# Prices of TensorE products taken from the trace, and new order offsets, in the list scheduler of a two-layer hybrid backbone

## The chip, the cores and the metric

The kernel runs on one core of one Trainium2 chip. The metric is the time of one execution on the device in microseconds (us); the time before is the median of three runs. The profile shows one execution of the kernel. Its engines are called PE (TensorE's matrix products), PEld (its weight loads, which overlap the products), DVE (VectorE), ACT (ScalarE), POOL (GpSimd) and SP (SyncE, which here issues the transfers).

## The reference

A backbone of two layers over 512 latent tokens with a context of 256 tokens, of width 1024. Cut to what matters:

```python
h, hc = x, ctx
for i in range(2):
    sh1, sc1, g1, sh2, sc2, g2 = split(silu(c) @ mod_w[i] + mod_b[i], 6)
    a = rmsnorm(h, norm1_w[i]) * (1 + sc1) + sh1
    if i == 0:      # the context ac is modulated in the same way with c_ctx
        m = ab_mixer(a, ac, ...)
    else:
        m = hyena_mixer(a, ...)      # two gated long convolutions, through an FFT
    h = h + g1 * m
    u = rmsnorm(h, norm2_w[i]) * (1 + sc2) + sh2
    h = h + g2 * ((silu(u @ w1) * (u @ w3)) @ w2)      # 1024 -> 2816 -> 1024
return rmsnorm(h, final_norm_w)

# ab_mixer: p = a @ w_in, then four heads of a gated delta rule (GDN) and four of
# gated linear attention (GLA), in both directions, in chunks of 64 tokens:
lmat = strict_lower(kb @ k.T * decay) + eye(64)                 # GDN, per chunk
sol = triangular_solve(lmat, concat([v * beta, kb * exp(gc)]))
s_new = s * gl + kd.T @ (u0 - kcd @ s)                          # chunk after chunk
m = concat([norm(o_gdn) * silu(z), norm(o_gla) * silu(g)]) @ w_out
```

## The kernel before

All products keep nearly the accuracy of float32 although most of them run in a shorter format (float32r): `split` (line 763) writes an operand as a rounded part on ACT and the rest on DVE, by a subtraction, and `mm3` (768) makes three products out of one. So each product of a projection stands three times in the instructions, and each weight that comes from memory costs an ACT cast and a DVE subtraction before PE can use it (`wsplit` 787, `wslab` 793). Weights are cut into slabs of 128 columns; the products of a projection are 128x512 (latent tokens) and 128x256 (context tokens). The small products of the first layer, in the block inverses, the scans and the linear attention, stay in float32 and are 32x32 to 128x128.

The work is recorded in sections, each with a name. In the first layer the string `AB_ORDER` (84) gives the order of recording, and `step` in `ab` (1153) calls what belongs to each letter: `g` the gates, `n0` to `n3` the projections of the GDN heads (`gdn_in` 1276), `p0` to `p3` their preparation, `i0` the inverse of the triangular 64x64 blocks of heads 0 and 1 and `i2` that of heads 2 and 3 (`gdn_inverse` 1331, which builds 32x32 blocks on DVE and merges them on PE in `gdn_merge` 1365, by products of 32x32 and then of 64x64), `s0` to `s3` the scans over the chunks (`gdn_scan` 1436), `l0` and `l1` the projections of the linear attention for two heads each (1528), `h0` to `h3` its heads (`gla_head` 1564), and `z0` to `z7` the projections of the output gates. Ahead of the first layer come the modulation vectors (`mlp`, `modc`, `m00` and so on), the norms (`in`) and the filters of the long convolution (`f0` to `f3`). Behind it come `out` (the output projection, `proj_late` 1685), `ffn0`, `ffn0b`, the convolution layer (`p0h` to `p3h`, `v0h` to `v3h`, `hyout`), `ffn1` and `last`.

The recorded order is not the order of issue. The class `Recorder` (229) keeps every instruction as an operation with its sources. `cost` (374) gives each a duration, `schedule` (413) is a list scheduler: it walks through time, and whenever an engine is free it gives it that one of its ready operations with the longest chain of work behind it, shifted by an offset. The offsets stand in the table `BOOST` (33), in nanoseconds, one per section and one per section and engine; they were found by a search. `clock` (428), inside `schedule`, turns the cost of a PE operation into a duration by a model of PE's clock with two levels, full and half. Where this model sees PE idle for more than `KEEP` = 900 ns (223), `warm` (567) puts products of a tile of ones by itself there, 128x128 in float32; I call them fillers. `issue` (578) then issues everything in the order found. Each engine works off its own queue in that order, so an instruction that waits holds back all behind it on its engine. Since everything is issued at one place, every instruction of an engine has line 591 in the profile, and instructions are told apart by their shapes.

The model's price of a PE operation before:

```python
            c = n / 2.4 * (1 if f32r else 2 if name == "transpose" else 4)
            op.cost += c / 4 if "tile_position" in k and k["lhsT"].shape[0] == P else c
```

Here `n` is the number of columns. `tile_position` marks products that use only a part of PE's array, such as the 32x32 pieces.

## Time and profile before

| what | value |
|---|---|
| median of three runs | 1661.76 us (1657.3 to 1662.93) |
| span of the profiled execution | 1659.7 us |
| time of the profiled execution | the profile gives its span alone; it is 2.1 us under the median |
| PE products | 8760 |
| mean memory traffic (HBM) | 121 GB/s |
| granted PE clock, mean over the span | 0.972 |

The span is the time from the first to the last instruction of the profiled execution. The clock is given as a share of the full speed of 2.4 GHz, so 0.50 is the lower level of 1.2 GHz and a mean in between says for which share of a stretch each level held. Idle time of an engine is put down to the operation that released it last. In rows of single engines a group that is named by one shape may hold other shapes that follow it without a pause.

### The profile page before, as it was taken

How to read it: one execution, taken by the hardware profiler on the slowest of the kernel's cores; microseconds unless marked ns; L12 is line 12 of the kernel's file. 1: busy time of each engine (PE TensorE's matmuls, PEld its weight loads, DVE VectorE, ACT ScalarE, POOL GpSimd, SP SyncE). 2: the span in 40 equal slices, each digit the busy share in tenths (PEclk: the TensorE clock that was granted, in tenths of full speed). 3: DMA queues.
4: the chain of work that ended last, by engine and by line, in shares of the span. 5: the costliest groups of instructions: out<-in, count | busy, mean ns of one | idle time of the engine just before them, and what ended most of it. 6: DMA issues, size and time to landing. Idle time of an engine off the chain costs nothing.

```text
span 1659.7 us, 22542 instructions
## 1 busy us (share of the span) xinstructions
PE 1607.0 (97%) x8760; PEld 1307.0 (79%) x8760; DVE 992.3 (60%) x1584; ACT 631.3 (38%) x1021; POOL 311.9 (19%) x395
## 2 busy tenths in 40 slices
PE   7999999999998899999999999999999999999998
PEld 4677777889876677888878887888887788888886
DVE  4967885587668877333376376689885433333224
ACT  4555633752546334232323224334335332222223
POOL 0334525723333200000000000244340000000002
PEclk9999997999998799999999999999999999999999
DMA  8755351221111165333378493333432233334232
GB/s 295 244 164 166 116 181 55 59 71 52 46 42 48 45 190 177 98 93 99 92 250 267 137 294 108 105 109 96 139 97 76 81 97 92 99 89 140 89 93 85
DMA packets 237540, 202.40 MB, mean 122 GB/s; under 512 B 11038, under 2 KB 211672, under 8 KB 237433
## 3 DMA queue, kind: packets, MB, share of 16 engines
q1 hardware_dynamic: 237432, 200.96, 39.5%
q8 instruction: 69, 1.13, 0.3%
q14 instruction: 39, 0.31, 0.1%
HBM read 187.27 MB, written 13.66 MB: 121 GB/s over the span
## 4 chain that ended last, share of the span: by engine, by line
PE 81%; DVE 9%; DMA 4%; ACT 2%; issue 2%; POOL 1%; SPq 1%; POOLq 0%; DVEq 0%; ACTq 0%
PE bank L591 81%; DVE t L591 9%; ACT t L591 2%; DMA t<-in_mod_w_dram 2%; POOL t L591 1%; DMA t<-in_hy_filt_out_dram 1%; SPq L591 1%; DMA t<-in_dft_filt_dram 0%; DMA kscr<-t 0%; DMA t<-in_ctx_dram 0%; DMA t<-kscr 0%; ACT bank L591 0%; POOLq L2084 0%; ACT L584 0%; DVEq L591 0%
## 5 line engine op out<-in xcount | busy, mean ns | idle before, releaser
L591 PE MATMUL bank<-t 128*128 128x512 f32 (+6 forms) x8760 | 1607.0, 354 | 45.4 <-DVE t L591 24.3
L591 PEld LDWEIGHTS bank<-t 128*128 128x128 f32 (+4 forms) x8760 | 1307.0, 183 | 344.9 <-DVE t L591 40.7
L591 DVE TENSOR_TENSOR t<-t 128x512 fp32r<-128x512 f32 (+13 forms) x707 | 534.2, 783 | 331.9 <-ACT t L591 294.4
L591 ACT CAST t<-t 128x1024 fp32r<-128x1024 f32 (+3 forms) x411 | 320.7, 794 | 728.5 <-PE bank L591 610.6
L591 POOL TENSOR_TENSOR t<-t 128x256 f32<-128x256 f32 (+3 forms) x195 | 211.7, 1106 | 740.8 <-DVE t L591 375.0
L591 DVE TENSOR_TENSOR t<-bank,t 128x512 f32<-128x512 f32 (+6 forms) x229 | 108.1, 505 | 55.5 <-PE bank L591 48.5
L591 ACT ACTIVATE t<-t 128x512 f32<-128x512 f32 (+6 forms) x183 | 114.3, 649 | 60.4 <-DVE t L591 44.1
L591 POOL COPY t<-t 32x192 f32<-32x192 f32 (+3 forms) x96 | 47.0, 496 | 479.6 <-DVE t L591 458.5
L591 DVE SCALAR_TENSOR_TENSOR t<-bank,t 128x511 f32<-128x511 f32 (+3 forms) x160 | 95.9, 617 | 55.1 <-PE bank L591 45.5
L591 DVE SCALAR_TENSOR_TENSOR t<-t 128x1024 f32<-128x1024 f32 (+8 forms) x135 | 109.9, 845 | 17.8 <-DMA t<-in_mod_w_dram 13.5
L591 DVE TENSOR_TENSOR t<-t,bank 128x512 f32<-128x512 f32 x44 | 30.2, 687 | 133.0 <-PE bank L591 132.3
L591 ACT COPY t<-bank 128x256 f32<-128x256 f32 (+4 forms) x152 | 64.9, 448 | 102.0 <-PE bank L591 99.7
L591 ACT ACTIVATE t<-bank 128x512 f32<-128x512 f32 (+7 forms) x134 | 59.8, 456 | 80.0 <-PE bank L591 76.0
L591 ACT ACTIVATE t<-bank,t 128x512 f32<-128x512 f32 (+2 forms) x87 | 48.1, 568 | 34.8 <-PE bank L591 17.3
L591 DVE SCALAR_TENSOR_TENSOR t<-t,bank 64x128 f32<-64x128 f32 (+1 forms) x112 | 38.3, 345 | 19.4 <-PE bank L591 17.0
L591 DVE COPY t<-bank 128x256 f32<-128x256 f32 (+7 forms) x68 | 29.9, 451 | 22.6 <-PE bank L591 21.0
L584 ACT ACT_TABLE_LOAD x32 | 41.1, 1283 | 1.4 <-PEq L2076 0.8
L591 POOL TENSOR_SCALAR t<-t 128x128 f32<-128x128 f32 x40 | 28.7, 725 | 48.7 <-PE bank L591 22.2
L591 DVE TENSOR_SCALAR t<-t 128x1024 f32<-128x1024 f32 (+6 forms) x52 | 25.1, 496 | 12.5 <-PE bank L591 7.3
L591 POOL MEMSET t<- 32x192 f32 (+10 forms) x47 | 18.4, 395 | 60.2 <-DVE t L591 30.1
L591 DVE TENSOR_TENSOR_SCAN t<-t 64x768 f32<-64x768 f32 x8 | 14.0, 1751 | 0.2
L591 DVE STREAM_TRANSPOSE t<-t 128x1024 f32<-128x1024 f32 x6 | 10.5, 1801 | 3.1 <-DMA kscr<-t 3.0
(17 smaller groups left out, 45.2 us busy)
## 6 DMA issues: line engine op xcount, KB each, us to landing
t<-in_ffn_w_dram SPq DMA_DIRECT2D x126, 512.0 KB
t<-in_mod_w_dram SPq DMA_DIRECT2D x96, 512.0 KB
t<-in_ab_w_in_dram SPq DMA_DIRECT2D x28, 512.0 KB
t<-in_hy_w_in_dram SPq DMA_DIRECT2D x24, 512.0 KB
kscr<-t SPq DMA_DIRECT2D x72, 128.0 KB
t<-kscr SPq DMA_DIRECT2D x24, 256.0 KB
t<-gscr SPq DMA_DIRECT2D x8, 384.0 KB
t<-in_ffn_w_dram SPq DMA_DIRECT2D x8, 384.0 KB
```

Of the source, the lines that this page charges most:

```text
L584: s.nc.scalar.add_instruction(mybir.InstLoadActFuncSet(name=s.nc.get_next_instruction_name(), engine=mybir.EngineType.Activation, act_func ...
L591: r = getattr(getattr(s.nc, o.eng), name)(*[b(x) for x in a], **{n: b(x) for n, x in k.items()})
```

## The change

`cost` prices a PE operation by other formulas: a product costs at least the load of its weights, a float32 product counts as two passes, and the small products get prices of their own. In `schedule` the surcharge of 2.5 ns a call is gone (the new prices hold one). The table `BOOST` is new throughout. Five docstrings are removed, which moves no instruction. The operations recorded are the same 5950 with the same sources and the same places in memory; their order is another, and there are 86 fillers instead of 73 (at the start, before the first layer, 50 instead of 29; in the last heads of the first layer 14 instead of 16; behind the first layer 22 instead of 28).

```diff
-BOOST = {"c": 1100, "c@gpsimd": -8900, "c@sync": 7100, "dft": 4200, "dft@scalar": -1200, "dft@vector": -316700,
...
+BOOST = {"": -47100, "@gpsimd": -2500, "@vector": -12200, "c": -4400, "c@gpsimd": -76900, "dft": 118900,
...
@@ cost
             f32r = x is not None and not isinstance(x, View) and x.dtype == F32R
             if x is not None and not isinstance(x, View):
                 op.rows = min(op.rows, x.shape[0])
-            c = n / 2.4 * (1 if f32r else 2 if name == "transpose" else 4)
-            op.cost += c / 4 if "tile_position" in k and k["lhsT"].shape[0] == P else c
+            l = k["in_"] if name == "transpose" else k["lhsT"]
+            w = l.shape[0] if name == "transpose" else int(np.prod(l.shape[1:]))
+            load = w / 1.2 + 2.5
+            if name == "transpose":
+                c = max(load, n * 0.8868)
+            elif f32r:
+                c = max(load, n * 0.4434 + 4.5)
+            else:
+                c = 2.0 * max(load, n * 0.8868 + 4.5)
+            if "tile_position" in k:
+                if l.shape[0] == P:
+                    c = 0.4434 * n
+                else:
+                    c = max(64.0, 0.9 * (n + 64.0))
+            op.cost += c
@@ schedule
-                o.end = clock(t, c + 2.5 * len(o.calls), o.rows / 128.0)
+                o.end = clock(t, c, o.rows / 128.0)
```

**The order on PE, in the inverse of heads 0 and 1.** The next rows are PE's, in the first layer, at `i0`. Products of 32x32 and 64x64 are those of the inverse, 128x512 and 128x256 are the projection of head 2 (`n2`), 128x128 the scan of head 0 (`s0`). `bank_` names the PSUM bank that is written. Before:

```order
L591 MATMUL bank_62<-t 128x512 x15
L591 MATMUL bank_65<-t 32x32 x12
L591 MATMUL bank_63<-t 32x32 x12
L591 MATMUL bank_67<-t 32x32 x12
L591 MATMUL bank_65<-t 32x32 x18
L591 MATMUL bank_63<-t 32x32 x18
L591 MATMUL bank_67<-t 64x64 x6
```

Fifteen wide products come first, then 72 of 32x32 in one run. In the new order the inverse is in two pieces. Its first half is mixed with the projection:

```order
L613 MATMUL bank_60<-t 64x64 x6
L613 MATMUL bank_61<-t 128x512 x3
L613 MATMUL bank_67<-t 64x64 x6
L613 MATMUL bank_61<-t 128x512 x6
L613 MATMUL bank_66<-t 128x128
L613 MATMUL bank_60<-t 128x128
```

Ahead of these rows the pieces of 24 and 36 products of 32x32 have six wide ones between them. The second half is mixed with the scan's 128x128 products:

```order
L613 MATMUL bank_67<-t 128x128
L613 MATMUL bank_66<-t 128x128
L613 MATMUL bank_60<-t 32x32 x12
L613 MATMUL bank_65<-t 128x128
L613 MATMUL bank_64<-t 128x128
L613 MATMUL bank_67<-t 32x32 x18
L613 MATMUL bank_66<-t 128x128
L613 MATMUL bank_60<-t 128x128
L613 MATMUL bank_61<-t 128x512 x3
```

What moved: wide products that stood ahead of the inverse, or behind it, now stand between its pieces, and a part of the scan too.

**The order on PE, in the inverse of heads 2 and 3.** PE's rows at `i2`, with the same shapes; the 128x512 products are `l0`'s and the 128x128 ones the scan of head 2. Before:

```order
L591 MATMUL bank_66<-t 32x32 x18
L591 MATMUL bank_64<-t 64x64 x6
L591 MATMUL bank_66<-t 128x128
L591 MATMUL bank_61<-t 128x128
L591 MATMUL bank_66<-t 64x64 x6
L591 MATMUL bank_67<-t 128x128
L591 MATMUL bank_64<-t 128x128
L591 MATMUL bank_61<-t 64x64 x6
L591 MATMUL bank_66<-t 64x64 x6
L591 MATMUL bank_67<-t 128x128
L591 MATMUL bank_64<-t 128x128
L591 MATMUL bank_61<-t 128x512 x3
```

Now:

```order
L613 MATMUL bank_63<-t 64x64 x6
L613 MATMUL bank_61<-t 128x128
L613 MATMUL bank_66<-t 64x64 x6
L613 MATMUL bank_65<-t 128x512 x3
L613 MATMUL bank_63<-t 64x64 x6
L613 MATMUL bank_66<-t 128x128
L613 MATMUL bank_61<-t 128x128
L613 MATMUL bank_65<-t 128x512 x3
```

What moved: three wide products at a time come between the small ones, and a group of three 128x512 and three 128x256 stands between the earlier pieces, where none stood in the rows before until the last.

**The order on DVE, at the end of head 3 and in the linear attention's head 0.** In the next rows SCALAR_TENSOR_TENSOR 64x768 is a scan of head 0 (the trace calls it a scan too), TENSOR_TENSOR 128x512 the squares of head 3 for its norm, COPY 64x12 and 64x8 the boundary copies of head 0. Before:

```order
L591 TENSOR_SCALAR t<-bank_64 128x512
L591 TENSOR_SCALAR t<-bank_62 128x256
L591 SCALAR_TENSOR_TENSOR t<-bank_65,t 128x128
L591 SCALAR_TENSOR_TENSOR t<-t 128x768
L591 TENSOR_TENSOR t<-t 128x1024
L591 SCALAR_TENSOR_TENSOR t<-t 64x768 x2
L591 TENSOR_TENSOR t<-t 128x512
L591 COPY t<-t 64x12 x2
L591 COPY t<-t 64x8 x2
L591 TENSOR_TENSOR t<-t 128x768
```

Now:

```order
L613 TENSOR_SCALAR t<-bank_61 128x512
L613 TENSOR_SCALAR t<-bank_65 128x256
L613 TENSOR_TENSOR t<-t 128x512
L613 SCALAR_TENSOR_TENSOR t<-t 128x768
L613 TENSOR_TENSOR t<-t 128x1024
L613 SCALAR_TENSOR_TENSOR t<-t 64x768 x2
L613 COPY t<-t 64x12
L613 COPY t<-t 64x8
```

What moved: the squares of head 3 from behind the two scans of head 0 to ahead of them, and two copies of the four were taken apart.

## Rows read from the trace of the kernel before

In rows of a table by stretch the columns are the stretch, its length, the busy time and the number of instructions of PE, PEld, DVE, ACT and POOL, the granted PE clock, the busy share of the DMA engines, and GB/s. In a timeline they are the start, the length, the engine, line and operation (output, sources, shape, count), and in brackets the idle time ahead with its releaser. In groups by shape they are line, engine, operation, tiles, shape, count, then busy us, mean ns of one record, and the idle time ahead.

**Rows 1.** The head of the profile and the busy times of the engines.

```profile
span 1659.7 us, 22542 instructions
...
PE 1607.0 (97%) x8760; PEld 1307.0 (79%) x8760; DVE 992.3 (60%) x1584; ACT 631.3 (38%) x1021; POOL 311.9 (19%) x395
```

**Rows 2.** The table of stretches, all engines.

```profile
0.00:86.00 86.00, 73.94 (x497) 47.70 (x497) 60.33 (x140) 42.98 (x91) 18.04 (x26) 0.94 0.84 266
268.00:274.00 6.00, 6.00 (x152) 5.33 (x151) 4.74 (x8) 1.81 (x5) 4.35 (x13) 0.98 0.07 21
274.00:294.00 20.00, 20.00 (x184) 17.22 (x182) 7.16 (x14) 7.12 (x18) 7.12 (x16) 0.50 0.17 41
399.00:418.00 19.00, 18.10 (x334) 15.92 (x334) 8.93 (x13) 6.03 (x17) 11.19 (x29) 1.00 0.01 3
418.00:437.00 19.00, 16.82 (x105) 14.66 (x106) 9.70 (x23) 10.84 (x25) 9.48 (x14) 0.82 0.21 56
516.00:530.00 14.00, 14.00 (x37) 9.50 (x37) 10.32 (x20) 3.52 (x7) 0.09 (x1) 0.51 0.09 27
547.00:571.00 24.00, 19.65 (x92) 16.82 (x93) 19.40 (x46) 5.83 (x9) 4.73 (x4) 0.58 0.18 55
584.00:877.00 293.00, 291.74 (x1284) 233.17 (x1285) 149.81 (x164) 90.21 (x114) 0.00 (x0) 1.00 0.48 147
1286.00:1652.00 366.00, 365.64 (x1584) 295.96 (x1582) 123.11 (x141) 103.45 (x139) 10.77 (x7) 1.00 0.31 95
```

**Rows 3.** Timeline of PE, 250 to 585 us.

```profile
260.85 91.68 PE L591 MATMUL bank<-t 128*128 128x256 f32 x763 [1.36 <-DVE t L591]
...
418.48 0.49 PE L591 MATMUL bank<-t 128*128 128x128 f32 x2 [0.99 <-ACT t L591]
419.48 15.68 PE L591 MATMUL bank<-t 128*128 128x128 f32 x98 [0.51 <-ACT t L591]
...
458.23 17.36 PE L591 MATMUL bank<-t 128*128 128x128 f32 x127 [2.14 <-DVE t L591]
...
498.67 5.26 PE L591 MATMUL bank<-t 128*128 128x512 f32 x20 [1.19 <-DVE t L591]
...
537.42 4.63 PE L591 MATMUL bank<-t 64*128 64x128 f32 x28 [1.34 <-DVE t L591]
```

**Rows 4.** PE by shape: 268 to 274, 274 to 294, 399 to 418 us.

```profile
L591 PE MATMUL bank<-t 32*32 32x32 f32 x143 | 4.2, 194 | 0.0
L591 PE MATMUL bank<-t 128*128 128x512 f32 x9 | 2.3, 397 | 0.0
...
L591 PE MATMUL bank<-t 64*64 64x64 f32 x55 | 6.5, 316 | 0.0
L591 PE MATMUL bank<-t 32*32 32x32 f32 x102 | 5.5, 237 | 0.0
L591 PE MATMUL bank<-t 128*128 128x512 f32 x9 | 4.9, 681 | 0.0
L591 PE MATMUL bank<-t 128*128 128x128 f32 x18 | 4.8, 439 | 0.0
...
L591 PE MATMUL bank<-t 128*128 128x512 f32 x15 | 6.0, 429 | 0.0
L591 PE MATMUL bank<-t 128*128 128x256 f32 x15 | 4.2, 280 | 0.0
```

**Rows 5.** The table of stretches, a stretch of eight fillers and one of wide products alone.

```profile
30.00:33.57 3.57, 3.57 (x17) 3.57 (x17) 3.47 (x6) 1.64 (x4) 0.00 (x0) 0.50 1.02 397
705.00:747.00 42.00, 42.00 (x184) 34.28 (x183) 14.33 (x16) 12.74 (x16) 0.00 (x0) 1.00 0.32 94
```

**Rows 6.** Timeline of DVE, 490 to 500 and 530 to 585 us.

```profile
494.37 3.53 DVE L591 TENSOR_TENSOR_SCAN t<-t 64x768 f32<-64x768 f32 x2
...
532.46 0.96 DVE L591 TENSOR_TENSOR t<-t 128x768 fp32r<-128x768 f32 x1
545.89 2.38 DVE L591 TENSOR_TENSOR t<-t 128x768 fp32r<-128x768 f32 x1
```

More of the change, by code (lines that the diff above doesn't have):

```diff
@@ L32 @@
 CW = 256
-BOOST = {"c": 1100, "c@gpsimd": -8900, "c@sync": 7100, "dft": 4200, "dft@scalar": -1200, "dft@vector": -316700,
[5 rows of a table removed]
-         "g": 119000, "g@gpsimd": 1100, "g@scalar": -1900, "g@sync": -17900, "g@tensor": 5500, "h": -119600,
-         "h0": -2100, "h0@gpsimd": -54600, "h0@scalar": 24800, "h0@tensor": 1200, "h0@vector": 2700,
-         "h1@scalar": 34600, "h2": 4200, "h2@gpsimd": 145500, "h2@scalar": -3900, "h2@tensor": 22100,
-         "h3@gpsimd": 6800, "h@vector": -200, "ht@scalar": 11900, "ht@tensor": 89700, "hy": -14100,
-         "hy@sync": -12500, "hy@vector": 2100, "hyout@scalar": 26400, "hyout@sync": 4000, "hyout@tensor": 3400,
-         "hyout@vector": -38500, "i0@gpsimd": 17700, "i0@scalar": -30100, "i2@gpsimd": 1400, "i2@scalar": 57700,
-         "i2@vector": -87000, "in": -197200, "in@scalar": -13600, "in@sync": 146900, "in@tensor": -9300,
-         "in@vector": -3000, "l0": -3500, "l0@scalar": -9800, "l0@vector": 284400, "l1@tensor": -8400,
-         "last": 300600, "last@sync": 2900, "last@tensor": -41300, "last@vector": -30000, "m02": -22900,
[6 rows of a table removed]
-         "mlp@sync": -10700, "mlp@tensor": 29000, "modc": 40000, "modc@tensor": -900, "modc@vector": 36700,
[3 rows of a table removed]
-         "n3@vector": -96700, "out": -8800, "out@sync": -57800, "out@tensor": 180400, "p0": 6000,
[11 rows of a table removed]
-         "v3h@sync": -1700, "v3h@tensor": -4300, "vec": -24300, "vec@sync": -1400, "vec@vector": 110900,
[6 rows of a table removed]
@@ new lines @@
+BOOST = {"": -47100, "@gpsimd": -2500, "@vector": -12200, "c": -4400, "c@gpsimd": -76900, "dft": 118900,
+         "dft@scalar": 109600, "dft@sync": -35900, "dft@vector": -5600, "f0": -9100, "f0@scalar": -43000,
[10 rows of a table added]
+         "h@sync": 3400, "h@tensor": -23700, "h@vector": -87000, "ht": 90900, "ht@scalar": 9100, "ht@tensor": -52000,
+         "hy": -2500, "hy@scalar": 32600, "hy@sync": -11700, "hy@tensor": 3500, "hy@vector": 9800, "hyout": -39100,
+         "hyout@scalar": -56900, "hyout@sync": 6200, "hyout@tensor": 20000, "hyout@vector": -6100, "i0@gpsimd": 400,
[9 rows of a table added]
+         "m14@tensor": -19800, "m15@vector": -700, "mlp": 9500, "mlp@scalar": 33800, "mlp@sync": -10700,
+         "mlp@vector": -4500, "modc": 40000, "modc@sync": 800, "modc@tensor": -900, "modc@vector": 36700,
[4 rows of a table added]
+         "n3@tensor": 700, "out": -4600, "out@scalar": -65300, "out@sync": -6900, "out@tensor": 167200,
[15 rows of a table added]
+         "vec": -24300, "vec@scalar": -178700, "vec@sync": -1800, "vec@tensor": -44700, "vec@vector": 110900,
[6 rows of a table added]
```

75 rows, old and new, of the table BOOST are left out of this document.

## Prediction

> **What bounds the kernel now.** I read the page's head first. The reader is to see that TensorE (PE) is busy for 1607.0 of 1659.7 us [rows 1]. So a new order can only win in three ways: the 52.7 us without PE work, the time in which PE works at the lower of its two clock levels, and filler products that stand in somebody's way. The three runs shown have a median of 1661.76 us, 2.1 us above the span of the profiled execution; I sum against the span and add 2.1 at the end.
>
> The second view is the table of stretches [rows 2]. In the feed-forward blocks (584 to 877 us and 1286 to 1652 us) PE is busy for 291.74 of 293 and 365.64 of 366 us at a granted clock of 1.00, 2.4 GHz. There is nothing to win there, whatever the order. What is lost lies before 584 us, in the first layer. From 274 to 294 us PE is busy for all 20.00 us and the granted clock is 0.50, 1.2 GHz. From 418 to 437 us it is 0.82 on average, and near the end of the layer 0.51 (516 to 530 us) and 0.58 (547 to 571 us). A stretch of length L at a mean clock g holds only g x L us of full-speed work, so these four lose 10.0, 3.4, 6.9 and 10.1 us, about 30 us in all.
>
> The third view is PE's own timeline, where a bracket at a row's end is an idle time and its releaser. The waits that the change touches are 0.99 and 0.51 us for ScalarE (ACT) at 418 us, 2.14 and 1.19 us for VectorE (DVE) at 458 and 499 us, and 1.34 us at 537 us [rows 3]. The clock of 0.82 stands right behind the pair at 418 us. But at 274 us it fell with no wait at all, behind a run of 32x32 products.
>
> The fourth view tells what PE did in that stretch [rows 4]. A 128x512 product costs 42.00/184 = 0.228 us where nothing else runs [rows 5]; a 128x256 one I put at half of that and a little, 0.12 us. These I call wide. From 274 to 294 us there were 9 wide records, 2.05 us of the 10.0 us of full-speed work done; the rest is 32x32, 64x64 and 128x128 products in float32. From 399 to 418 us the small products of the second inverse had 15 of 128x512 and 15 of 128x256 among them, 5.2 of 19 us, and the clock stayed at 1.00. These two rows are the two cases between which I place the new order.
>
> **The change, part by part.** No instruction of the computation is added or removed; they are given out in another order. Only fillers differ: 86 products of the ones by themselves instead of 73.
>
> The first part is the block inverse of heads 0 and 1 (i0, beside s0 and n2). Before, 72 products of 32x32 stand in one run, from 268 to 274 us beside nine wide records [rows 2, 4]: 143 records (two a product) in 6.00 - 2.05 = 3.95 us, 0.055 us a product. Behind it the clock was 0.50 for 20 us. In that stretch 55 records of 64x64 were busy for 6.5 us [rows 4], so a product takes 0.24 us there and 0.12 us at full clock; for a 128x128 one I take a filler's 0.22 us (below). In the new order the first half of the inverse has 24 products of 128x512 and 9 of 128x256 among its small ones, 6.5 us of wide work beside 60 of 32x32 (3.3 us), 24 of 64x64 and 4 of 128x128 (3.8 us). That is more wide work than in the row at 1.00, so this half should run at 2.4 GHz. The second half has nine wide products (2.05 us) beside 60 of 32x32 (3.3 us), 24 of 64x64 and 16 of 128x128 (6.4 us). That is like the row at 0.50. If all its 11.7 us run at half clock, they lose 11.7 us instead of 10.0, that is +1.7; if none does, -10.0. Its last piece, 18 of 32x32, 24 of 64x64 and 10 of 128x128, has no wide product at all, 6 us. I take a loss of those 6 us: **-4 us**, between -10.0 and +1.7.
>
> The second part is the same inverse for heads 2 and 3 (i2, beside s2 and l0). Before, its last twelve rows ahead of l0's next products hold 18 of 32x32, 24 of 64x64 and 7 of 128x128 and no wide one, 5.4 us of work, and there stand both ACT waits and the clock of 0.82. ACT had a 128x1024 weight cast in its queue between the copies that PE wanted. Now l0's wide products stand between the pieces, none more than about 3 us from the next, and the cast comes later. The waits (1.50 us) and the clock (3.4 us) could go: -4.9 at most, 0 at least. I take **-4 us**, since the stretch now looks like the row from 399 to 418 us.
>
> The third part is DVE's queue. The 128x512 sum of squares of head 3 stood behind two scans; these took 3.53 us, the sum came after them, and PE waited 1.19 us for it [rows 3, 6]. It now stands ahead of the pair: **-1.2 us**, between that and 0. In the same way the step of head 3 for which PE waited 2.14 us loses a 128x1024 subtraction and a 128x512 step ahead of it in the queue, but fewer PE products now stand between it and its source: **-1 us**, between -2.1 and 0.
>
> The fourth part goes the other way. In the last heads (h1, h3) all of z2's products now come ahead of h1's. Nine of them, 2.05 us, cover the 1.34 us wait at 537 us and are missing behind it: 0. The 128x768 subtraction of a weight of the output projection moves from behind head 3's two boundary copies to ahead of them, right behind the scans. That shape took 0.96 us once and 2.38 us where GpSimd (POOL) worked beside it [rows 6]; POOL's product for head 3 needs what follows those copies, and PE needs that product. If the delay is not hidden, it costs 2.4 us, otherwise 0: **+1 us**.
>
> The fifth is the fillers. The first layer's start has 21 more. Eight fillers took 3.57 us at half clock, 0.45 us each [rows 5], so 0.22 us at full; the 21 cost between 0 and 9.4 us. I cost them at nothing, since in the first 86 us the DMA engines are 84% busy and PE has 12 us without work [rows 2]; the first 50 loads keep their order but for two neighbours, and what PE waits for there is a load. If that cover were gone, they would cost the 9.4 us. Behind the first layer there are six fewer, 1.3 us at most: 0. In the f3 section products stand a little closer behind their DVE subtraction, where PE waited 1.36 us already [rows 3]: between 0 and +1.4, 0 taken.
>
> Sum: -4 - 4 - 1.2 - 1 + 1 = -9.2 us. 1659.7 - 9.2 = 1650.5 us of span, and with the 2.1 us **1652.6 us**, 0.55% below the median.
>
> **The rivals.** First, that the mix does not matter to the clock and only waits do. For it speaks the clock of 0.82 behind the pair of waits; against it, the 20.00 busy us out of 20 at 0.50 [rows 2]. Then the first part is worth 0, the second 1.5, and the sum is -1.5 - 1.2 - 1 + 1 = -2.7 us: 1659 us, no change. The Trainium skill (TensorE: Matmul & The Clock Gate, section "What's actually happening") has a rule of this kind: the gate is set by how busy PE has been of late, so an engine that never pauses should keep 2.4 GHz whatever it multiplies. By that rule the mix would bring nothing and the time would be this rival's 1659 us; the trace disagrees with it, by the row at 274 us.
>
> Second, on the other side: small products with wide ones strewn among them keep a low clock low, and do so all along instead of in one piece. Its places are the two inverses. The nine wide records between 274 and 294 us did not lift the clock [rows 4]. If it is low when i0 begins to mix, the second half (11.7 us of work) and a third of the first (4 us) run at half clock and lose 15.7 instead of 10.0; if the same happens in i2, its 22 us of work lose up to 22 instead of 3.4, 18.6 more. With half of this second price, and nothing else gained, the time is 1659.7 + 5.7 + 9.3 + 2.1 = 1677 us. It decides when the clock falls before the mixed stretch begins, at a wait or at the first 32x32 products. Against it stands that from 399 to 418 us the clock held.
>
> Third, that the change does more than it says: the fillers. If the 21 at the start are on the path at half clock, the sum is -9.2 + 9.4 = +0.2 us, 1662 us. Against it stands the DMA share of 0.84 [rows 2].
>
> **How the numbers follow.** The forecast has a chance of 0.48, the first rival 0.20, the second 0.24, the third 0.08. A measurement of this kernel tells about 0.3% from no change, 5 us, so faster means below 1656.8 and slower above 1666.7. The forecast's own range, with the bounds of its terms, is 1641 to 1660 us; nine tenths of it are faster (0.43). The first rival reaches below 1656.8 in a quarter of its cases (0.05). Faster is 0.48; slower is the second rival, 0.24; 0.28 is left for no change. The last heads lose 17.0 us at low clock [rows 2], which I leave as it is; if they win a part of that, the low end is 1638. At the high end the range goes into the second rival, to 1672. This leaves out some 2 in 10.
>
> **What would show it.** The stretch that holds i0 should have a granted clock of 1.00 in its first half, and less than 20 us at 0.50 in all; in i2 there should be no wait of 0.99 us and no clock below 1.00; the wait of 1.19 us for DVE ahead of head 3's closing product should be gone. The feed-forward blocks should take the same 293 and 366 us within 2. The forecast is wrong if the time at the lower clock before 584 us does not shrink by at least 10 us, or if new waits of PE for DVE in the last heads take it back.

## The result, and the profile after

The changed kernel takes 1716.47 us (median of four runs, 1710.34 to 1724.07), 1.0321 times the kernel before, interval 1.026 to 1.0381. The kernel before, with one more run beside it, has a median of 1662.35 us. So the change costs 54 us, where a time of 1652.6 us with a range to 1672 was predicted. The head of the changed kernel's profile, whose span is 1709.0 us:

```profile
span 1709.0 us, 22614 instructions
...
PE 1632.9 (96%) x8786; PEld 1325.9 (78%) x8786; DVE 1002.8 (59%) x1584; ACT 630.7 (37%) x1021; POOL 306.8 (18%) x395
...
L613 PE MATMUL bank<-t 128*128 128x512 f32 (+10 forms) x8786 | 1632.9, 357 | 68.3 <-DVE t L613 44.3
```

Against [rows 1], PE is busy for 26 us more and, by the last row, waits for 68.3 us. The same row of the kernel before says 45.4:

```profile
L591 PE MATMUL bank<-t 128*128 128x512 f32 (+6 forms) x8760 | 1607.0, 354 | 45.4 <-DVE t L591 24.3
```

The instructions are the same in another order, so I compare stretches of equal work. I give each PE product its full-speed time (the new price formula; fillers count nothing), 1499 us in all, and cut both traces where the same amount is done. In the text below, "at 300 us of work" means that point. Six stretches that differ follow, first of the kernel before and then of the changed one (columns as in [rows 2]; the last three rows of the second are pieces at the lower clock):

```profile
82.00:104.90 22.90, 22.32 (x155) 18.29 (x154) 14.98 (x47) 9.68 (x26) 5.68 (x10) 1.00 0.58 180
230.80:286.10 55.30, 51.90 (x465) 42.90 (x464) 37.64 (x86) 18.02 (x46) 27.19 (x50) 0.83 0.30 93
389.80:455.60 65.80, 62.27 (x666) 56.78 (x665) 38.98 (x74) 28.25 (x61) 26.77 (x50) 0.95 0.14 38
455.60:568.50 112.90, 98.67 (x543) 79.58 (x541) 87.84 (x167) 54.17 (x83) 39.14 (x34) 0.84 0.16 47
858.20:898.90 40.70, 40.70 (x188) 32.45 (x188) 32.19 (x33) 11.01 (x14) 0.00 (x0) 1.00 0.91 302
1084.10:1249.20 165.10, 163.40 (x979) 143.38 (x978) 143.31 (x210) 66.83 (x99) 69.59 (x77) 1.00 0.37 107
```

```profile
81.80:111.40 29.60, 27.03 (x164) 21.40 (x162) 15.34 (x50) 11.95 (x31) 8.63 (x13) 0.88 0.72 224
239.80:300.00 60.20, 56.69 (x435) 45.84 (x433) 39.42 (x85) 17.67 (x43) 29.00 (x55) 0.77 0.27 86
406.10:496.60 90.50, 78.65 (x670) 70.41 (x668) 49.90 (x89) 30.70 (x66) 34.39 (x56) 0.77 0.13 37
496.60:600.00 103.40, 90.72 (x531) 75.34 (x530) 83.07 (x158) 46.80 (x73) 30.29 (x29) 0.89 0.16 48
893.10:940.90 47.80, 41.97 (x190) 32.34 (x189) 38.99 (x39) 12.20 (x16) 0.00 (x0) 0.96 0.94 312
1127.50:1298.60 171.10, 164.54 (x971) 142.74 (x970) 146.36 (x206) 64.95 (x98) 65.32 (x72) 1.00 0.35 104
...
273.50:294.00 20.50, 20.50 (x151) 16.83 (x150) 6.38 (x10) 5.14 (x13) 8.72 (x21) 0.50 0.11 30
417.00:434.00 17.00, 16.89 (x186) 14.60 (x186) 5.67 (x7) 1.71 (x6) 9.36 (x24) 0.50 0.12 33
434.00:451.00 17.00, 17.00 (x152) 15.31 (x152) 2.46 (x5) 3.21 (x10) 5.47 (x12) 0.50 0.00 1
```

The reader should see, row by row: +6.7 us among filters and gates; +4.9 at i0; **+24.7** from the inverse of heads 2 and 3 to the linear attention's first head; -9.5 in the last heads; +7.1 at the change from `ffn0` to `ffn0b`; +6.0 in the convolution layer. The stretches that are not shown bring the other 9 us of the 49, some 6 of them at f2 (160 to 214 us). The row with +24.7 has 8.3 us more without PE work (11.85 for 3.53), and by its clock some 15 us of the rest (0.23 x 78.65 against 0.05 x 62.27). The timeline of PE has the new waits; its idle times in brackets belong to the places named above:

```profile
271.44 28.90 PE L613 MATMUL bank<-t 32*32 32x32 f32 x272 [1.12 <-DVE t L613]
...
417.11 36.49 PE L613 MATMUL bank<-t 32*32 32x32 f32 x358 [4.85 <-DVE t L613]
455.66 14.81 PE L613 MATMUL bank<-t 64*64 64x64 f32 x98 [2.06 <-ACT t L613]
...
489.12 3.18 PE L613 MATMUL bank<-t 128*128 128x128 f32 x14 [2.86 <-DVE t L613]
...
578.69 1.66 PE L613 MATMUL bank<-t 64*128 64x128 f32 x10 [4.73 <-DVE t L613]
...
934.57 10.66 PE L613 MATMUL bank<-t 128*32 128x256 f32 x44 [2.74 <-DVE t L613]
```

The wait of 4.85 us stands ahead of the first 32x32 product of heads 2 and 3. The kernel before has 0.69 us there:

```profile
399.24 4.91 PE L591 MATMUL bank<-t 32*32 32x32 f32 x126 [0.69 <-DVE t L591]
```

By shape, PE from 417 to 434 us, and then the lines that [rows 4] leaves out of 399 to 418 us of the kernel before:

```profile
L613 PE MATMUL bank<-t 32*32 32x32 f32 x144 | 7.5, 237 | 4.8 <-DVE t L613 4.8
L613 PE MATMUL bank<-t 128*128 128x512 f32 x9 | 6.1, 683 | 0.0
L613 PE MATMUL bank<-t 128*128 128x256 f32 x9 | 3.7, 415 | 0.0
L613 PE MATMUL bank<-t 64*64 64x64 f32 x24 | 3.1, 316 | 0.0
...
L591 PE MATMUL bank<-t 32*32 32x32 f32 x240 | 7.8, 192 | 0.7 <-DVE t L591 0.7
L591 PE MATMUL bank<-t 64*64 64x64 f32 x60 | 4.1, 222 | 0.2 <-ACT t L591 0.2
L591 PE MATMUL bank<-t 128*128 128x128 f32 x4 | 0.9, 300 | 0.0
```

There are 18 wide records to 168 small ones in the changed kernel, 0.11. From 399 to 418 us of the kernel before there were 30 to 304, 0.10. So it is nearly the same mix, at 0.50 in the one and at 1.00 in the other.

### The profile page after: what moved, and what is told of

It is laid out like the page before. It is cut to its first block, busy times and chain, and to the rows that moved or that the text cites. A ratio compares the mean times of both kernels' runs of the same rounds, so it can differ in the third digit from the quotient of the medians.

```text
span 1709.0 us, 22614 instructions
## 1 busy us (share of the span) xinstructions
PE 1632.9 (96%) x8786; PEld 1325.9 (78%) x8786; DVE 1002.8 (59%) x1584; ACT 630.7 (37%) x1021; POOL 306.8 (18%) x395
## 4 chain that ended last, share of the span: by engine, by line
PE 69%; DVE 15%; DMA 7%; ACT 4%; issue 2%; POOL 2%; SPq 0%; POOLq 0%; DVEq 0%; ACTq 0%
PE bank L613 69%; DVE t L613 15%; DMA t<-in_mod_w_dram 3%; ACT t L613 3%; DMA t<-in_ffn_w_dram 2%; POOL t L613 2%; DMA kscr<-t 1%; DMA t<-in_hy_filt_out_dram 1%; DMA t<-gscr 0%; DMA t<-kscr 0%; SPq L613 0%; DMA t<-in_dft_fwd_dram 0%; ACT L606 0%; ACT bank L613 0%; DMA t<-in_ab_w_in_dram 0%
## 5 line engine op out<-in xcount | busy, mean ns | idle before, releaser
L613 PE MATMUL bank<-t 128*128 128x512 f32 (+10 forms) x8786 | 1632.9, 357 | 68.3 <-DVE t L613 44.3
L613 PEld LDWEIGHTS bank<-t 128*128 128x128 f32 (+6 forms) x8786 | 1325.9, 186 | 374.9 <-DVE t L613 61.7
L613 DVE TENSOR_TENSOR t<-t 128x512 fp32r<-128x512 f32 (+16 forms) x707 | 543.7, 796 | 348.0 <-ACT t L613 301.7
L613 DVE TENSOR_TENSOR t<-bank,t 128x512 f32<-128x512 f32 (+5 forms) x229 | 108.2, 504 | 71.1 <-PE bank L613 59.0
L613 ACT ACTIVATE t<-t 128x512 f32<-128x512 f32 (+7 forms) x183 | 114.6, 649 | 64.3 <-DVE t L613 50.0
L613 POOL COPY t<-t 32x192 f32<-32x192 f32 (+3 forms) x96 | 45.4, 479 | 490.5 <-DVE t L613 468.6
L613 ACT ACTIVATE bank<-t 128x512 f32<-128x512 f32 x8 | 4.8, 600 | 18.2 <-POOL t L613 16.3
```

The costliest lines, as they stand in the source:

```text
L613: r = getattr(getattr(s.nc, o.eng), name)(*[b(x) for x in a], **{n: b(x) for n, x in k.items()})
```

## The experiments

In the kernels under "Which part of the change" the scheduler runs with other prices or offsets. All others have the order of issue written out as a list (`replay` puts it in the place of `schedule`). BEFORE and AFTER are the two orders, `splice` issues the first up to so many us of work and then what is left in the order of the second, and `put` puts fillers ahead of operations, which are named by their numbers. Each kernel has one trace, from one of its runs.

**Where the time is lost**

```diff
-    order = k.nc.schedule()
+    order = splice((BEFORE, 485), (AFTER, END))
```

> The old order up to the first third of the output projection (some 485 us of full-speed product work), the new order behind it. Theory 'the losses are local, each where the new order stands': against the trace of the changed kernel, which reaches this point 33.4 us later than the kernel before and loses 15.5 us more behind it, this kernel should take 1662 + 15.5 = 1677 us, with no loss before the cut. Rival 'the losses behind the first layer come of the late arrival there' (loads and sums of modulation rows that have piled up): what is lost behind the cut goes too, and the time is within 4 us of the kernel before, 1662 us.

Measured: 1679.47 us, 1.012 (1.0066 to 1.0173), so what is lost behind the cut is local. The two places that lose most there:

```profile
858.80:909.80 51.00, 44.88 (x191) 34.15 (x190) 39.40 (x39) 12.30 (x16) 0.00 (x0) 0.90 0.90 296
1096.60:1267.40 170.80, 164.34 (x971) 142.53 (x970) 146.18 (x206) 64.83 (x97) 65.16 (x72) 1.00 0.35 105
```

The first is 10 us longer than 40.70, where the changed kernel lost 7.1; the second is 5.7 longer than 165.10, where it lost 6.0.

```diff
+    order = splice((AFTER, NOT_M1), (BEFORE, ONLY_M1))      # sections m10 to m15
```

> The new order, with only the instructions of the modulation of the second layer (sections m10 to m15: 48 loads of 512 KB, their sums on DVE, two products each on PE) moved back, on every engine, to where they stood in the old order between the other instructions. Theory 'pile': the loss of 7 to 10 us at the change from the first feed-forward block's first half to its second (880 to 940 us) comes of five of these sections standing within 52 us of product work instead of 160, so that DMA and DVE are full and PE waits behind them. Then PE should have no wait above 1 us there, and the kernel should gain 7 to 10 us on the changed one's 1710 to 1716: 1702 to 1708 us. Rival 'feed-forward order': the new order of the weight loads of the block itself is late; the waits stay and the time is within 4 us of the changed kernel.

Measured: 1711.73 us, 1.03 (1.0244 to 1.0356), no gain that the interval shows. The place named did recover, but the next stretch paid for it:

```profile
894.30:936.30 42.00, 41.13 (x188) 32.20 (x187) 32.28 (x33) 11.06 (x14) 0.00 (x0) 1.00 0.89 294
936.30:1066.30 130.00, 124.59 (x554) 98.27 (x554) 71.03 (x89) 40.47 (x51) 0.00 (x0) 0.99 0.57 177
...
1012.50 31.83 PE L732 MATMUL bank<-t 128*128 128x512 f32 x140 [2.88 <-DVE t L732]
```

The first took 42.0 instead of 47.8 us, but the second 130.0 instead of 125.3. The pile is the cause at 893 us. With the sections put back, PE waited 2.88 us, still in `ffn0b`, for DVE, which had itself waited 3.00 us for a load of modulation weights: a loss moved. "Pile" was right about the place and missed the time (1702 to 1708 us); the rival had the time, within the noise, and was wrong about the place.

**Which part of the change**

```diff
 # price_only: before.py with
-            c = n / 2.4 * (1 if f32r else 2 if name == "transpose" else 4)
...
+                c = max(load, n * 0.4434 + 4.5)
...
 # scale92: after.py with
-            op.cost += c
+            op.cost += 0.92 * c
 # others: after.py with
+        if eng != "tensor":
+            op.cost = c0 + 1.1 * (op.cost - c0)
```

`offsets_only` is the reverse of `price_only`; `wide_new` has the new price for float32r products alone, `small_new` for all but these.

> The new prices of PE's operations with the old table of offsets. Theory 'offsets are fitted to the prices they were searched with': new prices under old offsets throw the order about and the kernel is slower than both, above 1720 us. Rival 'the prices are the part that helps, the offsets the part that harms': at or below the kernel before, 1640 to 1665 us.

> The new table of offsets with the old prices. The new prices alone gave 1715 us with the old offsets, nearly the changed kernel's time. Theory 'slack': the old prices make PE look 7 to 8% faster in wide products (213 + 2.5 ns for 128x512 where the new ones say 231.5) and a third faster in 32x32 ones than it is, so the scheduler sees PE wait for DVE and ACT and starts their work earlier than the chip needs it; that lead is what keeps PE fed and its clock up. Then these offsets, with the old prices, give 1662 to 1685 us. Rival 'fit': only prices and offsets that were found together make a good order; then 1700 us or more.

> The changed kernel with every PE price multiplied by 0.92, which brings the wide products to 213 ns, their old price, and leaves the small ones dear against them. Theory 'slack': 1662 to 1690 us, and in the inverse of heads 2 and 3 no wait above 2 us for DVE. Rival 'fit': above 1716 us, since these offsets were not found with these prices. Rival 'dear small products': their new price against the wide ones is what reorders the inverse, so nothing changes: 1700 to 1725 us.

> The changed kernel, with the new price for float32r products alone; float32 products, transposes and the pieces of PE's array at their old prices. Theory 'slack': wide products are most of PE's time, so most of the loss is here: 1695 to 1720 us. Rival 'dear small products': 1660 to 1685 us.

> The changed kernel, with float32r products at their old price and the small ones at the new. Theory 'slack': 1662 to 1690 us. Rival 'dear small products': 1700 to 1725 us.

> The changed kernel, new prices and new offsets, with the prices of all DVE, ACT, POOL and issue operations raised by a tenth. Theory 'slack': truthful prices of PE alone take away the lead that the other engines had; with theirs raised too, PE waits less: the idle time that the changed kernel has over the kernel before (22.9 us; 4.9 of it in the convolution layer, between 940 and 1100 us of product work) falls to under 12 and under 2 us, as with the old price of the wide products (3.8 to 11.9 and 0.1 to 1.6), and the time to 1680 to 1705 us. Rival 'fit': offsets that were not found with these prices; waits stay above 20 us and the time is 1710 us or more.

| kernel | wide price | offsets | median us | ratio (interval) | PE idle us | fillers |
|---|---|---|---|---|---|---|
| before | old | old | 1662.35 | 1 | 45.4 | 73 |
| changed | new | new | 1716.47 | 1.0321 (1.026 to 1.0381) | 68.3 | 86 |
| price_only | new | old | 1714.79 | 1.032 (1.0244 to 1.0396) | 69.2 | 102 |
| wide_new | new | new | 1742.04 | 1.0458 (1.0355 to 1.0561) | 79.0 | 133 |
| offsets_only | old | new | 1696.37 | 1.0184 (1.0051 to 1.0317) | 51.1 | 141 |
| scale92 | old (all x 0.92) | new | 1695.99 | 1.0182 (1.0078 to 1.0285) | 49.1 | 171 |
| small_new | old | new | 1703.43 | 1.0226 (1.0121 to 1.0331) | 57.3 | 140 |
| others | new, other engines x 1.1 | new | 1700.52 | 1.024 (1.0196 to 1.0284) | 54.0 | 165 |

The idle times are those of the first row of the costliest groups in each profile, as in these of `price_only` and `scale92`:

```profile
L604 PE MATMUL bank<-t 128*128 128x512 f32 (+9 forms) x8818 | 1632.2, 356 | 69.2 <-DVE t L604 38.5
```

```profile
L613 PE MATMUL bank<-t 128*128 128x512 f32 (+7 forms) x8956 | 1635.9, 354 | 49.1 <-DVE t L613 30.9
```

The last six kernels have two runs each. The new prices alone bring the whole loss. The new offsets make no difference on top of them, but with the old prices they alone cost 1.8%.

PE's idle time goes with its price against that of the other engines: the three kernels with wide products at their new price wait 68 to 79 us, the four in which PE is cheaper against the rest 49 to 57. But these four have 140 to 171 fillers, which the scheduler puts where its model sees PE idle. With 0.22 us a filler, the prediction's estimate from [rows 5], idle time and fillers together are 61 us in the kernel before, 87 in the changed one, 92 and 108 in `price_only` and `wide_new`, and 82 to 90 in the four. So the waits were filled more than they were shortened (in the convolution layer, `others` waits 2.1 instead of 6.6 us and has 5.9 us of fillers; 170 us either way).

None of the theories holds as it stands. "Slack" met its time in `others` alone (1680 to 1705 us), and missed it in `offsets_only`, `scale92`, `wide_new` and `small_new`. "Dear small products" had the time of `small_new` and missed `wide_new`, the slowest of all with the small products at their old price, by 57 us. "Fit" missed its bounds in `price_only`, `offsets_only`, `scale92` and `others`; what is left of it is that no pair but the old prices with the old offsets had a median under 1695 us.

**What lets the clock fall**

```diff
 # i2_before
+    order = splice((AFTER, 300), (BEFORE, END))
 # i2_before_fill: the same, and ahead of the first 32x32 product of i2
+    order = put(order, {2060: 14})      # operation: fillers ahead of it
```

> The new order up to some 300 us of full-speed product work, just ahead of the inverse of heads 2 and 3, and the old order from there to the end. Theory 'local': the 24.7 us lost between 406 and 497 us in the inverse and scan of heads 2 and 3 go, the 9.6 us won in the last heads go too, and what the new order lost before the cut stays: 1662 + 16 = 1678 us. The clock should then be at 1.00 through the inverse of heads 2 and 3 as before. Rival 'the clock is low there because of what came earlier': some 34 us at 0.50 are still there, and the time is near 1695 us.

> The spliced order of the earlier run (new up to 300 us of product work, old behind), with 14 fillers in PE's wait of 3.27 us ahead of the first 32x32 product of heads 2 and 3. That run had 27 us at 0.50 behind this wait in the same order of products that ran at 1.00 in the kernel before, behind a wait of 0.69 us. Theory 'the wait lets it fall, the mix holds it down': with the wait covered the stretch runs at 1.00 for its first 17 us, as in the kernel before, and the kernel takes 9 to 14 us less than the 1690 us of that run: 1676 to 1683 us. Rival 'the place is at the edge whatever stands ahead': the clock falls again within 7 us, and the gain is under 4 us.

Measured: 1693.68 us, 1.0166 (1.0107 to 1.0225), and 1685.37 us, 1.0138 (1.0083 to 1.0194). The first has the rival's time, not the 1678 us of "local"; the second missed its 1676 to 1683 us by 2. As whole times the two can't be told apart; the stretch tells their traces apart. Without fillers:

```profile
420.81 9.95 PE L732 MATMUL bank<-t 32*32 32x32 f32 x139 [3.27 <-DVE t L732]
...
421.50:438.50 17.00, 17.00 (x184) 14.68 (x183) 3.81 (x6) 1.71 (x6) 7.95 (x25) 0.50 0.01 2
```

With them:

```profile
410.88 4.94 PE L732 MATMUL bank<-t 32*32 32x32 f32 x126 [0.20 <-DVE t L732]
...
410.90:427.90 17.00, 16.84 (x314) 14.82 (x315) 7.05 (x11) 4.92 (x14) 10.53 (x28) 1.00 0.01 2
```

It is the order of products that ran at 1.00 in the kernel before. Behind 3.27 us of waiting it ran at 0.50, with that wait covered at 1.00 again: 184 records in 17 us, then 314.

These are two single executions, and that of the second took 1669.68 us where its other runs took 1677.69 to 1694.08. The other traces bear on it, and they do not all agree. With the old order of products here and at most 0.72 us of waiting ahead, `before`, `early_before` and `best` ran at 1.00 for the first 18 us and more; with that wait filled, `covered` did too, and `covered_lift` but for 3.4 us. `mix` (below) had the same products and the same wait as the kernel before, and fell after 6 us:

```profile
412.50 4.92 PE L732 MATMUL bank<-t 32*32 32x32 f32 x126 [0.69 <-DVE t L732]
...
418.70:435.80 17.10, 17.10 (x148) 14.61 (x146) 3.34 (x6) 1.99 (x6) 4.78 (x13) 0.50 0.01 1
```

In the new order and in those of the other prices, the clock had fallen within 7 us in all eleven traces: in eight behind 0.9 us or more, in three (`fill`, `after_covered`, `small_new`) behind waits of 0.73 us at most. So neither the wait nor the products settle it alone. That the wait of 3.27 us let the clock fall in `i2_before` is likely and not shown.

In the inverse of heads 0 and 1 the traces do not agree. These are the 40 us from its first 32x32 product on, of the kernel before and `best` (the old order, no wait right ahead), then of the changed kernel and `i2_before_fill` (the new order, waits of 1.12 and 1.01 us):

```profile
270.00:310.00 40.00, 40.00 (x445) 35.22 (x445) 17.70 (x35) 18.53 (x43) 17.97 (x35) 0.74 0.09 21
268.70:308.70 40.00, 40.00 (x512) 36.03 (x512) 24.78 (x47) 23.91 (x54) 27.78 (x50) 1.00 0.17 50
271.40:311.40 40.00, 39.95 (x426) 33.31 (x426) 17.72 (x32) 13.22 (x33) 17.36 (x36) 0.74 0.12 34
273.10:313.10 40.00, 38.24 (x480) 32.61 (x481) 23.19 (x44) 21.86 (x48) 24.32 (x44) 1.00 0.15 41
```

Nothing was edited there, and each order ran at 0.50 for 20.5 us in one execution and at 1.00 throughout in another. So one order with one wait can take either level in the first inverse; what decides it there stays open.

```diff
 # unmix: five groups of l0's wide products ahead of i2's first product
-    2060, 2063, 1884, 2066, 2070, 2074, 1885, ...
+    1884, 1885, 1886, 1887, 1888, 2060, 2063, 2066, 2070, ...
 # mix: the 72 products of 32x32 of i0 broken up by n2's and n3's wide ones
-    1417, 1418, 1419, 1420, 1421, 1314, 1317, 1354, 1320, 1324, 1328, 1422, ...
+    1417, 1418, 1419, 1314, 1420, 1317, 1354, 1421, 1320, 1422, 1324, 1423, ...
```

> The old order, with the five groups of l0's wide products (3 of 128x512 and 3 of 128x256 each, some 1 us) that stand between the pieces of the inverse of heads 2 and 3 moved ahead of its first 32x32 product. Theory 'the mix holds the clock up once it is up': with the wide products gone the clock falls within the inverse, as it did in the inverse of heads 0 and 1, and stays at 0.50 for 14 to 24 us; loss 4 to 10 us less the 0.7 us wait that is covered, 1664 to 1671 us. Rival 'only waits let it fall': 1.00 through the inverse, and the time of the kernel before or 1 us less, 1658 to 1662 us.

> The old order with two pieces rewritten by hand. In the inverse of heads 0 and 1 the run of 72 products of 32x32 is broken up: a group of three 128x512 products stands behind each piece, eight of them, and then one group of n3's wide products behind every second piece. In the inverse of heads 2 and 3 five ACT operations of l0 come behind the copies that PE waits for. Theory 'the mix holds the clock up where it is up': the 20 us at 0.50 behind 274 us shrink to under 8, and the stretch from 160 to 200 us of product work loses 5 to 9 us of the 9 to 10 that it lost to the clock; the waits of 0.99 and 0.51 us shrink: 1662 - 8 = 1652 to 1658 us. Rival 'small products let it fall at this point whatever is among them, as in the changed kernel': the low stretch is as long as before and the time is 1660 to 1666 us.

Measured: 1671.38 us, 1.005 (1.0016 to 1.0084), and 1686.9 us, 1.0159 (1.0126 to 1.0193). `unmix` did what "the mix holds" said, with no wait above 0.15 us ahead of the fall:

```profile
412.70:436.60 23.90, 23.52 (x239) 21.49 (x240) 10.03 (x17) 8.23 (x22) 8.98 (x21) 0.50 0.16 45
```

`mix` did the opposite of my expectation. PE came to the inverse earlier and waited 0.95 us for it, the clock fell among the mixed products and, with new waits between them, was low for 41 us in three stretches up to 320 us, not for 20. Its second edit, on ACT, won nothing: the stretch of the other inverse took 75.0 us instead of 65.8, with a wait of 2.04 us for ACT. The first low stretch, and that of the second edit:

```profile
268.50:285.60 17.10, 17.10 (x151) 13.10 (x145) 5.47 (x9) 3.24 (x9) 4.90 (x13) 0.50 0.01 2
403.10:478.10 75.00, 70.44 (x665) 63.68 (x664) 39.19 (x75) 28.27 (x61) 25.93 (x50) 0.82 0.11 33
```

Since the first inverse takes either level unedited, what `mix` did to the clock there is one trace's word.

**Fillers in the waits**

```diff
 # fill
+    order = put(AFTER, {989: 4, 1314: 4, 2060: 20})
 # lift: inside the inverses
+    order = put(AFTER, {1328: 12, 2074: 12})
 # after_covered: twenty waits
+    order = put(AFTER, {2060: 20, 2564: 20, 2353: 12, 2114: 9, ...})
 # covered: twelve waits of the old order; covered_lift adds 1328: 12
+    order = put(BEFORE, {2060: 2, 2156: 4, 2161: 2, 1915: 5, 2353: 9, 2426: 5,
+                         2493: 4, 2519: 8, 2558: 5, 2625: 8, 2635: 8, 2662: 3})
```

> The new order with fillers in three of PE's waits: 4 ahead of a product of the filters at 266 us, 4 ahead of the first 32x32 product of heads 0 and 1 at 271 us, 20 ahead of the first 32x32 product of heads 2 and 3 at 417 us (4.85 us of waiting at 0.23 us a filler). Theory 'state': a wait lets the clock fall, and small products mixed with wide ones hold whichever clock they find. Then the stretch after 417 us, 34 us at 0.50, runs at 1.00 for most of its length and the kernel gains 10 to 17 us: 1700 to 1706 us. In the first inverse, at 271 us, the gain is 0 to 10 us more. Rival 'mix': the products there cannot hold 2.4 GHz whatever stands ahead; the clock falls within some 7 us of the first 32x32 product and the gain is under 4 us.

> The new order with 12 fillers inside each of the two low stretches: ahead of the first 64x64 products of the two inverses (278 and 425 us). At 0.50 the 12 cost 5.4 us. Theory 'state': the block lifts the clock and the mix behind it then holds 1.00; the second stretch is low for some 14 us instead of 34, the first for some 10 instead of 20, so that 10 + 5 us are won and some 10 paid: 1708 to 1716 us. Rival 'mix': the clock falls again behind the block, or does not rise, and the time is 5 to 11 us longer than that of the changed kernel, 1721 to 1727 us.

> The changed kernel with 128 fillers in twenty of its waits between 169 and 600 us. Theory 'the waits let the clock fall': the 14 us that it lost to the clock against the kernel before shrink to under 4 us, and the time to 1695 to 1703 us; the idle time turns into fillers and is not won back. Rival 'the new order's mix lets it fall': the low time stays within 10 us of the changed kernel's and so does the time, 1708 to 1716 us.

Measured: 1709.24 (1.0269, 1.022 to 1.0318), 1712.75 (1.0294, 1.0245 to 1.0342) and 1716.44 us (1.0306, 1.0252 to 1.036): none is clearly faster than the changed kernel. `fill` spoke against "state": three short waits (0.36, 0.73 and 0.16 us) were left among the first pieces, and the clock fell at 422.5 us for 20.5 us. `after_covered`, with the same fillers and almost the same waits there, fell 6 us behind the first 32x32 product too. So the rival, that the new order's products cannot hold 1.00 there, is not excluded, and how short a wait may be among these pieces stays open. `lift` spoke for "state":

```profile
409.90:423.60 13.70, 13.70 (x154) 12.72 (x151) 3.71 (x4) 1.71 (x6) 7.38 (x18) 0.50 0.15 41
423.60:443.00 19.40, 17.10 (x231) 14.77 (x229) 7.32 (x13) 5.83 (x15) 7.53 (x18) 1.00 0.00 1
...
398.80:485.80 87.00, 74.84 (x695) 67.24 (x693) 49.87 (x89) 30.70 (x66) 34.37 (x56) 0.86 0.14 39
```

Behind the block the mix ran at 1.00, past a wait of 0.51 us and until one of 2.06 us for ACT. But the whole stretch took 87.0 us instead of 90.5, and 88.4 in `after_covered` at a clock of 0.87:

```profile
407.50:495.90 88.40, 83.06 (x766) 75.22 (x764) 51.07 (x89) 30.58 (x66) 34.65 (x56) 0.87 0.15 43
```

The higher clock gave back 7 to 8 us (0.23 x 78.65 less 0.14 x 74.84, and less 0.13 x 83.06), and the stretch became 2 to 3.5 us shorter. The fillers' own time took the rest: in `lift` 12 of them, 2.6 to 5.4 us by [rows 5], while PE was idle for 12.2 us as against 11.9; in `after_covered` 48, some 11 us, for 6.5 us less of idle time.

```diff
 # best
+    order = splice((BEFORE, 362), (AFTER, 445), (BEFORE, END))
```

> The old order up to 362 us of full-speed product work (458 us in the trace of before), the new order up to 445 us of it (572 us; the last heads of the linear attention and the gates), the old order behind. In the traces with the new order in this place the stretch took 7 to 10 us less than before, 103 to 106 us for 113. Theory 'local': 1662 - 8 = 1652 to 1655 us, faster than both kernels. Rival 'the clock's path into it decides': the stretch takes 111 to 115 us as before and the time is within 3 us of the kernel before.

Measured: 1665.38 us, 1.0023 (0.9988 to 1.0058). The last heads in the new order took 113.7 us behind the old one, where they take 103.4 in the changed kernel; "local" fell. In these traces the gain there comes only with the new order ahead of it.

> The old order with 63 fillers in twelve of PE's waits between 398 and 575 us, about as many in each as fit at 0.23 us (2 for 0.51 us, 9 for 2.14 us). Theory 'the wait lets it fall': of the 22 us that the low stretches behind these waits lose (3.4 at 421 us, 1.7 at 458, 6.8 at 516, 3.4 at 547, 6.8 at 557) half to three quarters come back, at a cost of 2 to 5 us where a filler stands in the way: 1648 to 1655 us, faster than both kernels. Rival 'the fall has other grounds, or fillers only move it': within 4 us of the kernel before, or slower by what the fillers take.

> The same with 12 more fillers inside the inverse of heads 0 and 1, ahead of its first 64x64 product, where the clock falls behind 72 products of 32x32 without a wait. In the changed kernel such a block lifted the clock within 6 us and the mix behind it stayed at 1.00. Theory 'the block lifts, the rest holds': the low stretch of 20 us shrinks to 7 to 10 us, worth 5 to 6.5 us, for 4 to 5 us of fillers: 0 to 2 us less than the run without them. Rival 'it falls again behind the block': 4 to 6 us more than the run without them.

Measured: `covered` 1653.42 us, **0.9953 (0.9925 to 0.9981)**, faster than both kernels; `covered_lift` 1659.63 us, 0.9975 (0.9947 to 1.0002), not told from the kernel before. The two stretches of `covered`:

```profile
387.30:452.00 64.70, 62.20 (x691) 57.33 (x690) 39.11 (x74) 28.16 (x61) 26.64 (x50) 1.00 0.13 38
452.00:561.10 109.10, 100.82 (x637) 85.58 (x635) 87.62 (x166) 54.40 (x83) 38.60 (x33) 0.92 0.16 49
```

In this trace the clock goes from 0.95 to 1.00 and from 0.84 to 0.92, and 1.1 and 3.8 us are won. `covered_lift` took 6 us more than `covered`, as the rival said. Its low stretch in the first inverse was 6.9 us, but the work that took 55.3 us in the kernel before took 55.4: the block cost what the clock gave.

## Why the prediction was wrong

**The inverses (the first and second part).** The step that failed is "that is more wide work than in the row at 1.00, so this half should run at 2.4 GHz", and for i2 "the stretch now looks like the row from 399 to 418 us". I made the share of wide products the cause of the clock. It does not decide: nearly the same share stood at 1.00 before and at 0.50 after, and one order of products ran at either level, at 1.00 in `before` and at 0.50 in `i2_before`, behind a longer wait, and in `mix`, behind the same. `unmix` speaks, in one trace, for wide products counting while the clock is up. What decides stays open. In i2 the low stretch was 34 us instead of 7. In i0 it was 20.5 us as before, but there other executions of the same orders had none, so neither the 20 us that I read nor the +4.9 us is shown to be the order's. The sign that I gave, 10 us less at the lower clock before 584 us, did not come: by the mean clocks of 0.92 over 584 us and 0.91 over the 617 us of the same work, it went from some 93 (2 x 0.08 x 584) to some 111 us (2 x 0.09 x 617). The second rival, by which small products strewn with wide ones stay at a low clock, is what the trace shows at i2, with its deciding point, "at a wait or at the first 32x32 products". I gave it 0.24 and, for i2, half of its price, 9.3 us; the clock alone cost some 15 us there, the waits 8.3.

**A wait that I did not look for.** I read from the order what stands between products, and not when DVE's substitution ends against PE's arrival. Three of l0's wide groups stood ahead of i2's first product and one does now; the others are among the pieces. PE waits 4.85 us there instead of 0.69. The first rival, by which only waits count, would have needed this too. That this wait brings the 34 us at 0.50 is not shown: `fill` covered it, and the clock still fell.

**What I costed at nothing.** "There is nothing to win there, whatever the order" is right of the feed-forward blocks and I read it as "nothing moves". I asked only whether they keep their 293 and 366 us and put no price on losing cover. At the end of `ffn0` the sums of five modulation sections, with 512 KB loads, now stand within 80 us of work in the order of issue, where they had 156 (the 52 of the expectation for `mods` is not that of all five), at a DMA share of 0.94 against 0.91, and PE waits up to 2.74 us for DVE: +7.1. The convolution layer lost 6.0 us, of which 4.8 are waits for DVE. The filters lost some 12, to waits and to the clock (0.88 for 1.00 in the first row). These are 25 of the 49 us, and none was in the sum or in a rival. The first feed-forward block took 298 us by the same cut, not 293 within 2. The middles of the blocks did keep their pace (319.4 us from 1381.8 us on, 319.8 before).

**What held.** The fillers at the start cost nothing that shows (81.8 us for 82.0 in these two traces; the last section has the spread). The wait of 1.19 us ahead of head 3's closing product is gone [rows 3]. Head 3's step does not win 1 us: its wait grew from 2.14 to 2.86. The last heads won 9.5 us where I had +1, in spite of a wait of 4.73 us in h1 and with a clock of 0.89 for 0.84. I had not foreseen that gain, and its size is not firm: the same work, unedited, took 108 to 115 us in six traces with the old order and 104 to 108 in four with the new one from the start. One sum of mine does not come out: the bounds of the terms give some 1642 to 1667 us and not 1641 to 1660.

**Why measured prices gave a worse order.** Shown is that the new prices alone bring the whole loss, and that the new offsets alone cost 1.8 of the 3.2%. That the old prices were a lead in disguise, as I supposed, is not shown: with PE cheaper against the rest, a quarter to two fifths of the loss went (13 to 20 of 54 us), but waits and fillers together hardly did. That the old offsets fit only the prices they were found with is argued, by elimination. Of the 49 us between the two spans, 23 are time without PE work, 14 the clock (0.036 x 1632.9 against 0.028 x 1607.0) and some 2 to 3 fillers; the last 10 weren't traced.

## What to carry to other kernels

Before crediting a new order with a better mix of products, find for each place where the mix matters when its first operand arrives and what wait PE meets there. Price cover that is lost as well as cover that is won: an engine that is busy for 99% has nothing to gain from an order and everything to lose. Making one engine's prices truer in a list scheduler is a change of all orders at once (raising the others' by a tenth as well won back 16 of 54 us here), so try the order on the chip before you trust its model. When a scheduler may fill its waits, count waits and fillers together. And before one trace is called the effect of an edit, look at a place that was not edited.

## What was not expected of the hardware

The same order does not always get the same clock. Seven profiled kernels have the old order up to 82 us of the trace (40 us of work): the stretch took 80.4 to 90.8 us, with 3 to 12 us lost to the clock. Seven with the new order took 81.8 to 89.7 us. The first inverse ran at 0.50 for 20.5 us or not at all, as shown above. The kernel before itself took 1651.44 us at a granted clock of 0.979 and 1675.89 us at 0.960, so the 0.3% that I took for the noise was too little; how much of its spread comes from which place is not shown. The Trainium skill (TensorE: Matmul & The Clock Gate, section "What's actually happening") says that the same kernel shows other counts of slow products from run to run; these rows agree. The stretch at 417 us was busy for 16.89 of 17.00 us at 0.50. The same section of the Trainium skill says that how busy PE has been of late sets the gate; this row disagrees, as the one at 274 us did.
